# SSD stage of a hybrid encoder: ScalarE adds the decay differences, VectorE takes the minimum of four heads at once

## Chip, cores and metric

One core of a Trainium2 chip runs the whole program in one launch. The metric is device time in microseconds (us); lower is better. Engines are named as the profile names them: PE is TensorE (PEld its weight loads), DVE is VectorE, ACT is ScalarE, POOL is GpSimd, SP issues most DMAs.

## What is computed

Two layers on 1024 tokens of width 1024: dilated attention, then a bidirectional Mamba-2 SSD layer. The change lies in the SSD layer. For each of 8 groups (4 heads each) and each of 8 chunks (128 tokens each), with `acs` the running sum of `dt*a` inside a chunk, the reference does for each direction:

```
seg = acs_t[..., :, None] - acs_t[..., None, :]
decay = jnp.exp(jnp.where(lower, seg, -jnp.inf))
cb = jnp.einsum('bclgn,bcsgn->bcgls', cc, bc)
y_diag = jnp.einsum('bcgrls,bcsgrp->bclgrp', cb[:, :, :, None] * decay, xdt)
...
y_off = jnp.einsum('bclgn,cbgrpn->bclgrp', cc, prev) * jnp.exp(acs)[..., None]
```

The kernel handles both directions in one 128 x 128 matrix per head. The exponent is the smaller of the forward and the backward difference; each is the right one in its own triangle.

## The kernel before

**Work.** The main stream on PE is a dense projection: for each group six blocks (x0, x1, B, C, z0, z1) of 8 steps, each step six 128x512 matmuls (L376 to L378; each operand is split in a high part, cast by ACT in L271 into `whi`, and a low part, subtracted by DVE in L272 into `wlo`). A block accumulates in two of four PSUM banks `acc`. When it ends, ACT copies the two banks out with the convolution's middle tap (L1322), and DVE adds the other four taps (two instructions each, L1330), read from the same banks; only then are the banks free for the block after next. Later ACT applies silu (L1334).

**SSD items.** `ssd_items(g)` makes a list of small items, which `balance` weaves between the dense steps of the next group: A1 (PE transposes, L1403, copied out by ACT, L1405 and L1407), A2 (chunk states, L1415 to L1426), and for each chunk c from 7 down to 0: B0 (a DMA of the row sums into `acs`), B1(c), M(c) and, two chunks later, B2(c) (the output matmuls L1478, DVE L1482, POOL L1486). Each item carries a cost on PE and on DVE, and `balance` puts an item out when the DVE cost so far is small enough against the PE cost so far.

**B1(c)** of before: four DVE instructions make E (L1440: add a per-row scalar `delta`, take the minimum with the other direction's row sums); PE multiplies B by C (L1443); DVE masks the product into `cb` (L1446); ACT takes the exponential of E, head by head (L1448), scales `cb` into W, head by head (L1450), and takes the exponential of the row sums `acs` (L1452). **M(c)**: DVE adds the backward half into W (L1462, four instructions), multiplies E by W (L1464) and `acs` by C (L1467). After chunk 0 of a group ACT loads the table set for silu (L1454). Each engine runs its own instructions strictly in the order in which they are written.

Of the kernel before, what the change touches and what calls it, by code (L numbers as in the profile page):

```python
# [14 lines left out]
AF = mybir.ActivationFunctionType  # L15
OP = mybir.AluOpType
# [75 lines left out]
class Trunk:  # L92
# [1293 lines left out]
    def ssd_items(self, g):  # L1386
        nc = self.nc
# [6 lines left out]
        def ck(c):  # L1394
            return slice(P * c, P * c + P)
# [32 lines left out]
        def B0(c):  # L1428
            a = live["a", c] = self.u("acs", [P, 2, 4, P], F32, 4)
            nc.sync.dma_start(a, self.acsd[c, :, hs][None].to_broadcast([P, 2, 4, P]))  # L1430

        def dirs(c):

            return [d for d, k in ((0, c > 0), (1, c < C - 1)) if k]

        def B1(c):
            a = live["a", c]
            E, W = live["G", c] = self.u("E", [P, 4, P], F32, 3), self.u("W", [P, 4, P], F32, 2)
            for h in range(4):
                nc.vector.scalar_tensor_tensor(E[:, h], a[:, 0, h], self.delta[:, c, 4 * g + h:4 * g + h + 1], a[:, 1, h],  # L1440
                                               op0=OP.add, op1=OP.min)
            p = self.bank("a0", [P, P], 2)
            nc.tensor.matmul(p, st["B"][:, ck(c)], st["C"][:, ck(c)], start=True, stop=True)  # L1443
            cb = live["cb", c] = self.u("cb", [P, 2, P])
            tri = self.cst[:, CST["upper"][0]:CST["lower"][1]].rearrange("p (d l) -> p d l", d=2)
            nc.vector.tensor_mul(cb, p[:, None].to_broadcast([P, 2, P]), tri)  # L1446
            for h in range(4):
                nc.scalar.activation(E[:, h], E[:, h], AF.Exp, bias=self.nacb[:, c, 4 * g + h:4 * g + h + 1])  # L1448
            for h in range(4):
                nc.scalar.activation(W[:, h], cb[:, 0], AF.Copy, scale=self.dt[:, c, 4 * g + h:4 * g + h + 1])  # L1450
            ds = slice(dirs(c)[0], dirs(c)[-1] + 1)
            nc.scalar.activation(a[:, ds], a[:, ds], AF.Exp)  # L1452
            if c == 0 and g < 7:
                nc.scalar.preload_act_table_set(SILU)  # L1454

        def M(c):

            cb = live.pop(("cb", c))
            E, W = live["G", c]
            for h in range(4):  # L1460
                hh = 32 + 4 * g + h
                nc.vector.scalar_tensor_tensor(W[:, h], cb[:, 1], self.dt[:, c, hh:hh + 1], W[:, h],  # L1462
                                               op0=OP.mult, op1=OP.add)
            nc.vector.tensor_mul(E, E, W)  # L1464
            ds = dirs(c)
            a = live["a", c][:, ds[0]:ds[-1] + 1].rearrange("p d h l -> p (d h) l")
            nc.vector.tensor_mul(a, a, st["C"][:, None, ck(c)].to_broadcast([P, 4 * len(ds), P]))  # L1467

        def B2(c):

            y = self.bank("a3" if c % 2 else "a2", [P, 2, P])
            G, _ = live.pop(("G", c))
            ea = live.pop(("a", c))
            for r in range(2):
                mms = [(SS[6 - c if d else c - 1][:, d], ea[:, d]) for d in dirs(c)] + [(xt[c], G)]
                for k, (w, m) in enumerate(mms):
                    for i in range(2):
                        nc.tensor.matmul(y[64 * i:64 * i + 64, r], w[:, 2 * r + i], m[:, 2 * r + i],  # L1478
                                         start=k == 0, stop=k == len(mms) - 1)
            t = self.u("yt", [P, 2, P], F32, 2)  # L1480
            for r in range(2):
                nc.vector.scalar_tensor_tensor(t[:, r], st[f"x{r}"][:, ck(c)], self.sv[:, 2 * g + r:2 * g + r + 1],  # L1482
                                               y[:, r], op0=OP.mult, op1=OP.add)
            for r in range(2):
                z = st[f"z{r}"][:, ck(c)]
                nc.gpsimd.tensor_mul(z, z, t[:, r])  # L1486
            if c == 0 and g == 7:
                self.ylast = [st["z0"], st["z1"]]
            elif c == 0:
                for r in range(2):  # L1490
                    nc.gpsimd.dma_start(self.yd[2 * g + r], st[f"z{r}"])
# [7 lines left out]
        items = []  # L1499
# [6 lines left out]
        if g == 7:  # L1506
            items.append((1500, lambda: None, 0, 0))
        for c in range(C - 1, -1, -1):
            items.append((900, lambda c=c: B1(c), 0.25, 1.6))
            if c < C - 2:  # L1510
                items.append((500, lambda c=c: B2(c + 2), 1.7, 0.6))
            if c:
                items.append((1, lambda c=c: B0(c - 1), 0, 0))
            items.append((1150, lambda c=c: M(c), 0, 3.0))
# [273 lines left out]
```

## Time and profile before

| what | value |
|---|---|
| median of 3 runs | 1902.2 us (1900.9 to 1903.83) |
| the profiled execution | 1903.41 us, its span 1901.6 us |
| mean granted PE clock | 0.976 |
| busy share of the span | PE 94%, PEld 77%, DVE 75%, ACT 50%, POOL 17% |

The profile is of one execution. Busy shares are averages over stages with different limits. A wait in the trace is the idle time of an engine before an instruction, with the engine and line that ended it. "x4" behind a row means four instructions in a row, with the time from the first's start to the last's end. The SSD items run from about 1000 to about 1745 us; groups 1 to 5 look alike, about 93 us each, and the rows below are mostly of group 2.

### The profile page before, as it was taken

How to read it: one execution, taken by the hardware profiler on the slowest of the kernel's cores; microseconds unless marked ns; L12 is line 12 of the kernel's file. 1: busy time of each engine (PE TensorE's matmuls, PEld its weight loads, DVE VectorE, ACT ScalarE, POOL GpSimd, SP SyncE). 2: the span in 40 equal slices, each digit the busy share in tenths (PEclk: the TensorE clock that was granted, in tenths of full speed). 3: DMA queues.
4: the chain of work that ended last, by engine and by line, in shares of the span. 5: the costliest groups of instructions: out<-in, count | busy, mean ns of one | idle time of the engine just before them, and what ended most of it. 6: DMA issues, size and time to landing. Idle time of an engine off the chain costs nothing.

```text
span 1901.6 us, 28474 instructions
## 1 busy us (share of the span) xinstructions
PE 1790.2 (94%) x10050; PEld 1462.0 (77%) x10050; DVE 1428.1 (75%) x3220; ACT 955.5 (50%) x2095; POOL 330.1 (17%) x492
## 2 busy tenths in 40 slices
PE   5899999999999999999979999999999999888997
PEld 3678788777788887779868887878787877666787
DVE  8867568667664665566778898989898989878875
ACT  5454445444454545444435656464655555465632
POOL 4611122112211311000100101010101000233310
PEclk7899999999999999999989999999999999988998
DMA  6242234222311321355113232424232323244643
GB/s 254 87 130 81 81 107 134 85 86 83 105 52 54 81 60 49 91 188 169 63 45 99 85 100 78 100 78 101 78 110 80 106 83 91 89 129 127 199 155 101
DMA packets 99733, 193.65 MB, mean 102 GB/s; under 512 B 15624, under 2 KB 23048, under 8 KB 99592
## 3 DMA queue, kind: packets, MB, share of 16 engines
q1 hardware_dynamic: 86600, 167.32, 28.3%
q0 software_dynamic: 12288, 23.86, 4.5%
q8 instruction: 79, 1.29, 0.3%
q10 hardware_dynamic: 704, 0.66, 0.1%
q14 instruction: 62, 0.51, 0.1%
HBM read 169.00 MB, written 16.48 MB: 98 GB/s over the span
## 4 chain that ended last, share of the span: by engine, by line
PE 40%; DVE 7%; ACT 5%; issue 3%; DMA 2%; SPq 0%; DVEq 0%; POOL 0%; ACTq 0%; POOLq 0%
PE acc L376 8%; PE acc L378 7%; PE acc L377 7%; PE a L1478 3%; PE a L1416 2%; PE a L1002 2%; PE a L1000 2%; PE a L1001 2%; PE acc L1002 2%; PE acc L1001 1%; PE acc L1000 1%; DVE big L1330 1%; DVE wlo L272 1%; PE a L1403 1%; DMA acs<-acsd 1%
## 5 line engine op out<-in xcount | busy, mean ns | idle before, releaser
L376 PE MATMUL acc<-big,whi 128*128 128x512 f32 (+1 forms) x1520 | 632.7, 416 | 36.2 <-DVE big L1330 23.9
L377 PE MATMUL acc<-big,whi 128*128 128x512 f32 (+1 forms) x1520 | 597.3, 393 | 4.0 <-DVE big L294 4.0
L378 PE MATMUL acc<-big,wlo 128*128 128x512 f32 (+1 forms) x1520 | 597.2, 393 | 0.3 <-DVE wlo L272 0.3
L376 PEld LDWEIGHTS acc<-big,whi 128*128 128x128 f32 x1520 | 289.0, 190 | 103.7 <-issue 31.5
L378 PEld LDWEIGHTS acc<-big,wlo 128*128 128x128 f32 x1520 | 288.6, 190 | 64.8 <-DVE wlo L272 1.1
L377 PEld LDWEIGHTS acc<-big,whi 128*128 128x128 f32 x1520 | 290.1, 191 | 55.3 <-DVE big L294 7.5
L272 DVE TENSOR_TENSOR wlo<-wraw,whi 128x512 fp32r<-128x512 f32 (+1 forms) x298 | 216.8, 732 | 82.3 <-ACT whi L271 78.9
L271 ACT CAST whi<-wraw 128x512 fp32r<-128x512 f32 (+1 forms) x302 | 180.9, 611 | 86.1 <-PE a L1001 29.7
L695 ACT ACTIVATE sm<-sm,nb 128x256 f32<-128x256 f32 (+1 forms) x192 | 89.3, 466 | 198.3 <-DVE nb L693 195.7
L1448 ACT ACTIVATE E<-E,nacb 128x128 f32<-128x128 f32 x256 | 81.8, 391 | 200.2 <-DVE E L1440 200.2
L1486 POOL TENSOR_TENSOR big<-big,yt 128x128 f32<-128x128 f32 x128 | 68.0, 552 | 602.5 <-DVE yt L1482 547.5
L1330 DVE SCALAR_TENSOR_TENSOR big<-acc,cv,big 128x512 f32<-128x512 f32 (+1 forms) x248 | 170.9, 742 | 0.9 <-ACT big L1322 0.9
L706 DVE COPY pt<-a 128x512 f32<-128x512 f32 (+1 forms) x96 | 57.6, 600 | 76.5 <-PE a L704 76.5
L690 DVE CUSTOM_DVE_ANT_0 sm<-a,cst 128x256 f32<-128x256 f32 (+1 forms) x192 | 65.0, 376 | 62.4 <-PE a L685 62.0
L1001 PE MATMUL acc<-big,whi 128*128 128x512 f32 x224 | 91.4, 408 | 9.7 <-DVE big L1553 7.2
L1000 PE MATMUL a<-big,whi 128*128 128x256 f32 (+1 forms) x304 | 100.1, 329 | 0.0
L1002 PE MATMUL a<-big,wlo 128*128 128x256 f32 (+1 forms) x304 | 98.7, 325 | 0.7 <-DVE wlo L272 0.7
L1001 PE MATMUL a<-big,whi 128*128 128x256 f32 (+1 forms) x304 | 98.5, 324 | 0.0
L1002 PE MATMUL acc<-big,wlo 128*128 128x512 f32 x224 | 91.8, 410 | 4.6 <-DVE wlo L272 4.4
L1000 PE MATMUL acc<-big,whi 128*128 128x512 f32 x224 | 92.7, 414 | 1.2 <-ACT big L271 1.2
L592 POOL DMA_DIRECT2D rt<-kT x92 | 50.4, 561 | 249.4 <-ACT kT L532 149.9
L1462 DVE SCALAR_TENSOR_TENSOR W<-cb,dt,W 128x128 f32<-128x128 f32 x256 | 82.7, 379 | 7.3 <-ACT W L1450 6.6
(254 smaller groups left out, 3149.0 us busy)
## 6 DMA issues: line engine op xcount, KB each, us to landing
wraw<-in_win SPq DMA_DIRECT2D x186, 256.0 KB
acs<-acsd SPq DMA_DIRECT2D x64, 512.0 KB
wraw<-in_wout SPq DMA_DIRECT2D x112, 256.0 KB
big<-in_modw SPq DMA_DIRECT2D x48, 512.0 KB
yd<-big POOLq DMA_DIRECT2D x14, 512.0 KB, 3.5
big<-yd SPq DMA_DIRECT2D x28, 256.0 KB
vT<-mix POOLq DMA_DIRECT2D x20, 256.0 KB, 5.0
big<-in_xT SPq DMA_DIRECT2D x8, 512.0 KB
```

The costliest lines, as they stand in the source:

```text
L271: self.nc.scalar.copy(dst_hi, src)
L272: self.late.append((lambda: self.lo_engine.tensor_sub(dst_lo, src, dst_hi.bitcast(F32)), tile))
L376: mm(o, hi[:, cols], x_[:, t0:t0 + n], start=first, stop=False, **kw)
L377: mm(o, hi[:, cols], x_[:, H2 + t0:H2 + t0 + n], start=False, stop=False, **kw)
L378: mm(o, lo[:, cols], x_[:, t0:t0 + n], start=False, stop=last, **kw)
L695: nc.scalar.activation(sm[:, h, :W], sm[:, h, :W], AF.Exp, bias=nb[:, h:h + 1], scale=0.125, accum_out=stat[:, h, 1, i:i + 1])
L1000: mm(o, hi[:, c], x[:, t:t + n], start=kt == 0 and (n == H2 or m % 2 == 0), stop=False, **kw)
L1001: mm(o, hi[:, c], x[:, H2 + t:H2 + t + n], start=False, stop=False, **kw)
L1002: mm(o, lo[:, c], x[:, t:t + n], start=False, stop=kt == nkt - 1, **kw)
L1330: nc.vector.scalar_tensor_tensor(y[:, lo:hi], a[:, lo + o:hi + o], w[:, cv, k:k + 1], y[:, lo:hi], op0=OP.mult, op1=OP.add)
L1448: nc.scalar.activation(E[:, h], E[:, h], AF.Exp, bias=self.nacb[:, c, 4 * g + h:4 * g + h + 1])
L1462: nc.vector.scalar_tensor_tensor(W[:, h], cb[:, 1], self.dt[:, c, hh:hh + 1], W[:, h], op0=OP.mult, op1=OP.add)
```

## The change

The four DVE instructions of B1 that added and took the minimum become four ACT instructions that only add (`Identity` with a bias), and one DVE instruction that takes the minimum for all four heads. This minimum now stands behind the mask `cb` on DVE. On ACT the scaling into W now stands ahead of the exponential of E. The planner's DVE cost of B1 falls from 1.6 to 1.1.

```diff
@@ B1
             for h in range(4):
-                nc.vector.scalar_tensor_tensor(E[:, h], a[:, 0, h], self.delta[:, c, 4 * g + h:4 * g + h + 1], a[:, 1, h],
-                                               op0=OP.add, op1=OP.min)
+                nc.scalar.activation(E[:, h], a[:, 0, h], AF.Identity, bias=self.delta[:, c, 4 * g + h:4 * g + h + 1])
             p = self.bank("a0", [P, P], 2)
             nc.tensor.matmul(p, st["B"][:, ck(c)], st["C"][:, ck(c)], start=True, stop=True)
             cb = live["cb", c] = self.u("cb", [P, 2, P])
             tri = self.cst[:, CST["upper"][0]:CST["lower"][1]].rearrange("p (d l) -> p d l", d=2)
             nc.vector.tensor_mul(cb, p[:, None].to_broadcast([P, 2, P]), tri)
+            nc.vector.tensor_tensor(E, E, a[:, 1], op=OP.min)
+            for h in range(4):
+                nc.scalar.activation(W[:, h], cb[:, 0], AF.Copy, scale=self.dt[:, c, 4 * g + h:4 * g + h + 1])
             for h in range(4):
                 nc.scalar.activation(E[:, h], E[:, h], AF.Exp, bias=self.nacb[:, c, 4 * g + h:4 * g + h + 1])
-            for h in range(4):
-                nc.scalar.activation(W[:, h], cb[:, 0], AF.Copy, scale=self.dt[:, c, 4 * g + h:4 * g + h + 1])
@@ items
-            items.append((900, lambda c=c: B1(c), 0.25, 1.6))
+            items.append((900, lambda c=c: B1(c), 0.25, 1.1))
```

In the changed kernel L1440 is the ACT addition, L1445 the mask `cb`, L1446 the minimum, L1448 the scaling into W and L1450 the exponential of E; all other lines keep their numbers.

The planner's new cost moves items too. On ACT, in group 2 from the first chunk (c = 7) on, before:

```order
L1448 ACTIVATE E_11386<-E_11386,nacb_8966 128x128 x4
L1450 ACTIVATE W_11387<-cb_11394,dt_8962 128x128 x4
L1452 ACTIVATE acs_11288<-acs_11288 128x512
L1322 ACTIVATE big_11411<-acc_11280,cv_8789 128x512
L1322 ACTIVATE big_11411<-acc_11281,cv_8789 128x512
```

and after the change:

```order
L1322 ACTIVATE big_11408<-acc_11285,cv_8789 128x512
L1322 ACTIVATE big_11408<-acc_11286,cv_8789 128x512
L1440 ACTIVATE E_11411<-acs_11304,delta_8965 128x128 x4
L1448 ACTIVATE W_11412<-cb_11419,dt_8962 128x128 x4
L1450 ACTIVATE E_11411<-E_11411,nacb_8966 128x128 x4
L1452 ACTIVATE acs_11304<-acs_11304 128x512
```

The chunk's work on ACT has moved from ahead of the two copies of a block's end to behind them. For chunk 3 (L1440 right behind two L1322) and chunk 0 the order against L1322 is as before, with the four additions put in.

On DVE, at the same place, before:

```order
L1440 SCALAR_TENSOR_TENSOR E_11386<-acs_11288,delta_8965 128x128 x4
L1446 TENSOR_TENSOR cb_11394<-a_2085_11392,cst_71 128x256
L1462 SCALAR_TENSOR_TENSOR W_11387<-cb_11394,dt_8962,W_11387 128x128 x4
L1464 TENSOR_TENSOR E_11386<-E_11386,W_11387 128x512
L1467 TENSOR_TENSOR acs_11288<-acs_11288,big_11029 128x512
L1330 SCALAR_TENSOR_TENSOR big_11411<-acc_11280,cv_8789,big_11411 128x512
```

and after, where three further L1330 stand in place of the "...":

```order
L1445 TENSOR_TENSOR cb_11419<-a_2086_11417,cst_71 128x256
L1446 TENSOR_TENSOR E_11411<-E_11411,acs_11304 128x512
L1330 SCALAR_TENSOR_TENSOR big_11408<-acc_11285,cv_8789,big_11408 128x512
...
L272 TENSOR_TENSOR wlo_11444<-wraw_11216,whi_11443 128x512
L1462 SCALAR_TENSOR_TENSOR W_11412<-cb_11419,dt_8962,W_11412 128x128 x4
L1464 TENSOR_TENSOR E_11411<-E_11411,W_11412 128x512
L1467 TENSOR_TENSOR acs_11304<-acs_11304,big_11044 128x512
```

M(7) has moved behind the first four taps of the block and one L272.

At the end of the group ACT has, before:

```order
L1322 ACTIVATE big_11951<-acc_11837,cv_8789 128x512
L1448 ACTIVATE E_11954<-E_11954,nacb_8966 128x128 x4
L1450 ACTIVATE W_11955<-cb_11962,dt_8962 128x128 x4
L1452 ACTIVATE acs_11881<-acs_11881 128x512
L1454 ACT_TABLE_LOAD
```

and after:

```order
L1322 ACTIVATE big_11974<-acc_11859,cv_8789 128x512
L1440 ACTIVATE E_11977<-acs_11904,delta_8965 128x128 x4
L1448 ACTIVATE W_11978<-cb_11985,dt_8962 128x128 x4
L1450 ACTIVATE E_11977<-E_11977,nacb_8966 128x128 x4
L1452 ACTIVATE acs_11904<-acs_11904 128x512
L1454 ACT_TABLE_LOAD
```

Four additions have been put between the block's copy and the table load.

## Rows read from the trace of the kernel before

**Rows 1.** Busy time by stretch; columns PE, PEld, DVE, ACT, POOL, clock, DMA share, GB/s.
```profile
1200.00:1250.00 50.00, 48.47 (x297) 39.71 (x296) 47.27 (x104) 31.41 (x75) 5.03 (x10) 1.00 0.38 98
...
1700.00:1750.00 50.00, 42.98 (x264) 33.15 (x263) 48.51 (x87) 32.08 (x72) 25.17 (x22) 0.90 0.42 130
```

**Rows 2.** PE's waits from 1000 to 1750 us: total us, times, longest.
```profile
PE acc L376 <- DVE big L1330: 12.4, 8, 1.7
...
PE a L1403 <- ACT bt L1407: 6.8, 7, 1.2
```

**Rows 3.** Groups of instructions, 1000 to 1750 us: busy us, mean ns, idle before.
```profile
L1440 DVE SCALAR_TENSOR_TENSOR E<-acs,delta 128x128 f32<-128x128 f32 x256 | 76.6, 361 | 6.6 <-DMA acs<-acsd 6.6
...
L1464 DVE TENSOR_TENSOR E<-E,W 128x512 f32<-128x512 f32 x64 | 45.3, 707 | 2.2
```

**Rows 4.** Timeline of chunk 2, group 2: start us, us, engine, line; DVE, ACT, PE.
```profile
1237.06 1.13 DVE L1440 SCALAR_TENSOR_TENSOR E<-acs,delta 128x128 f32<-128x128 f32 x4
...
1239.12 1.35 DVE L1462 SCALAR_TENSOR_TENSOR W<-cb,dt,W 128x128 f32<-128x128 f32 x4
1241.11 1.22 DVE L1467 TENSOR_TENSOR acs<-acs,big 128x1024 f32<-128x1024 f32 x1
1242.25 1.40 DVE L1330 SCALAR_TENSOR_TENSOR big<-acc,cv,big 128x510 f32<-128x510 f32 x2
...
1237.52 1.28 ACT L1448 ACTIVATE E<-E,nacb 128x128 f32<-128x128 f32 x4 [6.00 <-DVE E L1440]
1238.70 1.27 ACT L1450 ACTIVATE W<-cb,dt 128x128 f32<-128x128 f32 x4
1239.88 1.05 ACT L1452 ACTIVATE acs<-acs 128x1024 f32<-128x1024 f32 x1
...
1243.14 0.47 PE L376 MATMUL acc<-big,whi 128*128 128x512 f32 x1 [1.53 <-DVE big L1330]
```

**Rows 5.** Timeline of DVE, chunks 7 to 3 of the same group; last row ACT.
```profile
1200.99 1.23 DVE L1462 SCALAR_TENSOR_TENSOR W<-cb,dt,W 128x128 f32<-128x128 f32 x4 [0.47 <-ACT W L1450]
...
1203.72 2.72 DVE L1330 SCALAR_TENSOR_TENSOR big<-acc,cv,big 128x512 f32<-128x512 f32 x4 [0.18 <-ACT big L1322]
...
1209.88 0.42 DVE L1446 TENSOR_TENSOR cb<-a,cst 128x256 f32<-128x256 f32 x1 [0.47 <-PE a L1443]
...
1215.05 1.14 DVE L1440 SCALAR_TENSOR_TENSOR E<-acs,delta 128x128 f32<-128x128 f32 x4
...
1221.24 1.13 DVE L1440 SCALAR_TENSOR_TENSOR E<-acs,delta 128x128 f32<-128x128 f32 x4
...
1226.52 0.69 DVE L272 TENSOR_TENSOR wlo<-wraw,whi 128x512 fp32r<-128x512 f32 x1
...
1232.51 2.71 DVE L1330 SCALAR_TENSOR_TENSOR big<-acc,cv,big 128x512 f32<-128x512 f32 x4
...
1226.26 1.46 ACT L1322 ACTIVATE big<-acc,cv 128x512 f32<-128x512 f32 x2 [0.65 <-PE acc L378]
```

**Rows 6.** Timeline of ACT and PE at the end of the group.
```profile
1255.62 1.45 ACT L1322 ACTIVATE big<-acc,cv 128x512 f32<-128x512 f32 x2 [6.58 <-issue]
1256.96 1.27 ACT L1448 ACTIVATE E<-E,nacb 128x128 f32<-128x128 f32 x4
...
1259.94 1.28 ACT L1454 ACT_TABLE_LOAD   x1
1261.23 2.95 ACT L1334 ACTIVATE big<-big 128x1024 f32<-128x1024 f32 x3
...
1264.24 0.66 PE L1403 MATMUL a<-cst,big 128*128 128x128 f32 x4 [0.32 <-ACT big L1334]
1266.13 1.02 PE L1403 MATMUL a<-cst,big 128*128 128x128 f32 x6 [1.23 <-ACT bt L1407]
```

**Rows 7.** Timeline of PE: one wait in group 6, one in group 7.
```profile
1605.60 0.47 PE L376 MATMUL acc<-big,whi 128*128 128x512 f32 x1 [1.75 <-DVE big L1330]
...
1675.10 0.50 PE L1002 MATMUL acc<-big,wlo 128*128 128x512 f32 x1 [2.48 <-DVE wlo L272]
```

## The prediction

> **What bounds the kernel now.** I read the busy time by stretch first, because the page's average (DVE 75%) mixes stages. In a middle group PE is busy 48.47 of 50 us, DVE 47.27 and ACT only 31.41; in the last group DVE is busy 48.51 and PE 42.98 [rows 1]. So in groups 1 to 5 (some 465 us) PE sets the pace, and a change on DVE or ACT counts only where PE waits; in the last two groups DVE sets it. Next the waits of PE. In the whole stage there are two kinds that matter: eight waits, 12.4 us, for a convolution tap (L1330) that frees a PSUM bank, and seven, 6.8 us, at the transposes that open the next group [rows 2]. Then the timeline of one middle group, to see what is late at each. The tap wait comes behind chunk 2: DVE reaches that tap at 1242.25, and PE, which had been waiting 1.53 us, starts at 1243.14 [rows 4]; groups 1 to 5 have one such wait each of about this size. The transposes wait for ACT: silu for 0.32 us, then the copies behind it for 1.23 us [rows 6]. The question is therefore not how busy DVE is, but when it reaches that tap, and when ACT reaches silu.
>
> **Cost of the operations.** The four DVE instructions take 1.05 us from the first to the mask behind them (the row's 1.13 us less the overlap of its end). Their mean over the stage is 361 ns each, idle not counted [rows 3]. The minimum of 128x512 is not in the trace; the nearest row is the product of E and W, two SBUF operands of the same size and type, 707 ns [rows 3], and about 0.61 us from its start to the next instruction when nothing interferes. I take 0.61; the bounds are 0.55 (half of an acs product, 1.14/2 [rows 4]) and 0.71. DVE is thus relieved of 0.44 us per chunk, 28 us over 64 chunks. The addition on ACT is a 128x128 activation with a bias, as the exponential is: four of those take 1.18 us (1237.52 to 1238.70 [rows 4]). ACT thus gets 64 times 1.18, 75 us, where it is idle for a third of the time. Both sums say little until one sees which chunks carry them to PE.
>
> **A chunk with nothing between B1 and M (chunks 5, 4, 2 and in part 3).** Before: DVE starts E at 1237.06, ACT its exponential 0.46 later, then W 1.18 later, and DVE can't add to the last head of W until ACT has it (the four take 1.35 instead of 1.13); it reaches the next work at 1242.25, 5.19 us after the start [rows 4]. After: from the mask, ACT starts W after 0.46 (the same handing over), the exponential 1.18 later, that of `acs` another 1.17 later, lasting 1.05; then 0.06 to hand over and 1.14 for the product with C: 5.06 us. DVE saves 0.44 us of work and mostly spends it waiting for ACT, since W has moved forward and the exponential backward in a chain of the same length. Gain 0.13 per such chunk. This needs the additions to be done in the ACT idle time that stands ahead (6.00 us here [rows 4]); without it they cost up to 1.18.
>
> A rule of the Trainium skill speaks for more than that: VectorE: DVE Perf Modes, section on the TRN2 errata, says that each SBUF instruction pays a fixed extra latency and that tiles of 512 elements or more should be used to spread it. The trace agrees that one 128x512 is cheaper than four 128x128 [rows 3]. By that rule alone the stage would give back 28 us of DVE; the second rival below takes it up from rows.
>
> **The tap wait, groups 1 to 5.** I follow DVE from the first tap of the block (1203.72 [rows 5]) to the tap on which PE waits. Chunk 7 now stands behind the block's copies on ACT: the additions end about 1203.2, so the minimum ends at 1203.85, and that first tap starts 0.13 later than before. Work of M(7), 2.4 us (1200.99 to 1203.72 less its pauses [rows 5]), now lies behind the taps instead of ahead: +2.4. The low part L272 waits for a cast that now comes after chunk 7: +0.15. Chunk 6 saves its 0.44 and the 0.47 that its mask waited for PE [rows 5]: -1.0 with rounding. Chunk 5 took 6.19 (1215.05 to 1221.24) with an L272 in it; now 0.61 + 5.06: -0.5. Chunk 4 took 5.28: -0.2 [rows 5]. Chunk 3 has the block's copies ahead of it on ACT (L1322 at 1226.26 [rows 5]), so its additions cannot be early: the chain on ACT, cast, copies, additions, W, two exponentials, makes 6.35 of its 5.99 (1226.52 to 1232.51 [rows 5]): +0.4. Chunk 2: -0.1. Sum +1.15: PE's wait grows from 1.5 to about 2.65. Lower bound: all gains of 0.44 come through and M(7) costs nothing, and the wait goes: -1.5. Upper bound: chunks 6 to 2 each pay half of the 1.18 as well: +4.
>
> **The end of a group.** Chunk 0 stands on ACT between the block's last copies, which wait for PE (1255.62), and the table load (1259.94 [rows 6]). The additions have no idle time ahead of them here. E starts at 1256.96 right behind the copies [rows 6], so the four additions push W, the exponentials, table load and silu by 1.18. W's place does not save anything, since only ACT's own order counts. PE's first wait grows from 0.32 to 1.5, and the second, behind the same ACT queue, stays 1.23: +1.17 in each of the five groups. The product that the last output matmuls need moves by about 0.4 us and has over 1 us in hand. Bounds: 0, if ACT had an unseen idle time, and 1.5.
>
> Groups 1 to 5 together: 5 x (1.15 + 1.17) = +11.6. Group 0 has neither wait of this size, and its last chunk has idle time ahead on ACT: 0.
>
> **Groups 6 and 7.** DVE sets the pace, and PE waits for it, 1.75 us at 1605.60 [rows 7]. In every other chunk of group 6, and in nearly all of group 7, taps or other DVE work lie between B1 and M and cover ACT's chain, so the whole 0.44 is gained. Group 6: its first chunk behind a copy costs 1.15, then three at 0.44, two at 0.13 and 0.5 for the short last one: -0.9. Group 7: the first chunk's additions stand in the ACT queue ahead of a cast whose low part PE already awaits (2.48 us at 1675.10 [rows 7]): +1.2; then six at 0.44: -2.6. Together -2.3, between -5 and +1.
>
> **Sum.** +11.6 - 2.3 = +9.3 us. The profiled execution took 1903.41 us (span 1901.6), 1.2 above the median of 1902.2; I add the change to the median: **1911 us**, 0.5% slower. Measured differences of this kernel tell from no change above about 0.2%, or 3.8 us.
>
> **Rivals.**
> *Forecast: a longer ACT queue costs more than DVE gives back.* 1904 to 1918. For it: the five group ends, where nothing can hide the additions. Against it: the tap term is a long sum of small shifts. Chance 0.55.
> *DVE's relief reaches PE.* If the 0.44 of five chunks or more arrives at the tap (2.2 is more than the 1.5 that PE waits), the eight tap waits go: -12.4 [rows 2]; groups 6 and 7 give -5; the group ends still cost up to +5.9. That gives 1885 to 1897. It decides from the point where the additions are always early and M(7) does not matter. Against it: the 5.06 us chain in a chunk, of which DVE's own work is the smaller part. Chance 0.20.
> *They cancel.* The tap wait stays at 1.5, the group ends cost 5.9 and the last groups give back 5: within 4 us of 1902. Chance 0.17.
> *ACT becomes the limit in each chunk.* If the additions are not early, because the row sums land late or the queue is never idle ahead, chunks 6 to 2 lose 0.5 each on top, 2.5 per group in five groups: 1923 or so. Against it: idle times of up to 6 us in the ACT rows. Chance 0.08.
>
> **How the numbers follow.** Slower by over 0.2%: forecast and last rival, 0.63. Same: 0.17. Faster: 0.20. The range runs from 1897 to 1919: it leaves out most of the second rival and the far end of the last, some 2 in 10. The likeliest case alone spans 1904 to 1918.
>
> **What would show it.** In the changed kernel's profile: four additions in 1.18 us and a minimum of about 0.61 to 0.7 us; waits of PE for L1330 of some 2.6 us in groups 1 to 5, sum near 18; waits of the transposes for silu near 1.5 us five times; DVE pauses before the products of M that end on ACT; an ACT addition that starts right behind L1322 at chunks 7, 3 and 0. I am wrong if the tap wait shrinks, if ACT is idle just ahead of chunk 0's additions at a group's end, or if the period of a middle group is not some 2 us above 93.

## The result, and the profile after

The changed kernel takes 1919.93 us (median of 4 runs, 1915.65 to 1925.54) against 1903.01 us for the kernel before on the same chip: ratio 1.0100, 95% interval 1.0074 to 1.0126. It is slower by 16.9 us, 0.9% of the median before, 8.9 us above the forecast of 1911 and 0.9 us above the upper end of the range. The profiled execution took 1915.65 us (span 1913.9, mean clock 0.975), the fastest of the four.

Busy time by stretch in the changed kernel, columns as in [rows 1]:

```profile
1200.00:1250.00 50.00, 47.64 (x293) 38.81 (x292) 43.40 (x84) 38.88 (x105) 4.60 (x10) 1.00 0.37 100
1700.00:1750.00 50.00, 43.24 (x270) 32.19 (x268) 46.46 (x79) 42.72 (x108) 26.43 (x21) 0.93 0.53 147
```

The relief of DVE is there: 47.27 us busy in the middle stretch became 43.40, 48.51 in the last became 46.46. PE did not get busier; in the middle stretch it fell from 48.47 to 47.64.

PE's waits of the changed kernel from 1000 to 1750 us (total, times, longest), and the groups of instructions that are new, moved or waiting (busy us, mean ns, idle before):

```profile
PE acc L376 <- DVE big L1330: 16.0, 6, 4.7
...
PE a L1403 <- ACT big L1334: 6.2, 10, 0.6
```

```profile
L1440 ACT ACTIVATE E<-acs,delta 128x128 f32<-128x128 f32 x256 | 81.6, 392 | 13.3 <-DMA acs<-acsd 13.3
...
L1446 DVE TENSOR_TENSOR E<-E,acs 128x512 f32<-128x512 f32 x64 | 44.2, 691 | 31.7 <-ACT E L1440 31.7
L1445 DVE TENSOR_TENSOR cb<-a,cst 128x256 f32<-128x256 f32 x64 | 26.8, 419 | 32.7 <-PE a L1442 32.7
```

The operations cost what was forecast: an addition 392 ns, the minimum 691 ns. But DVE now idles 31.7 us ahead of the minimum, for the additions, and 32.7 us ahead of the mask, for PE (11.8 before). Of PE's waits in [rows 2] those for the tap rose from 12.4 to 16.0 us: in groups 1 to 5 five waits of 1.54 became five of 2.26, and in group 6 three, 4.7 us together, became one of 4.66. Those for silu (L1334), 1.9 us before, are now 6.2.

**Where the time went.** I measure a group from one table load at a group's end (L1454) to the next. Before, group 2 took 92.65 us (1167.29 to 1259.94), after, 94.87 (1168.03 to 1262.90; groups 2, 4 and 5, without a fall of the clock, 94.87 to 94.93). In the profiled executions: up to the first L1344 (the table load that opens group 0), ahead of any changed instruction, -3.0 us; group 0, +2.0 (65.15 to 67.17); groups 1 to 5, +10.7 (466.6 to 477.3); group 6, +5.1 (87.04 to 92.11); from there to the end, -2.5. Sum +12.3, the difference of the spans.

Chunks 3 and 2 of group 2 in the changed kernel: ACT, DVE, PE. They answer to [rows 4, 5].

```profile
1227.38 1.44 ACT L1322 ACTIVATE big<-acc,cv 128x512 f32<-128x512 f32 x2
1228.71 1.27 ACT L1440 ACTIVATE E<-acs,delta 128x128 f32<-128x128 f32 x4
1229.88 1.27 ACT L1448 ACTIVATE W<-cb,dt 128x128 f32<-128x128 f32 x4
1231.06 1.27 ACT L1450 ACTIVATE E<-E,nacb 128x128 f32<-128x128 f32 x4
1232.23 1.05 ACT L1452 ACTIVATE acs<-acs 128x1024 f32<-128x1024 f32 x1
...
1228.74 0.42 DVE L1445 TENSOR_TENSOR cb<-a,cst 128x256 f32<-128x256 f32 x1
1230.01 0.69 DVE L1446 TENSOR_TENSOR E<-E,acs 128x512 f32<-128x512 f32 x1 [0.85 <-ACT E L1440]
...
1234.49 2.72 DVE L1330 SCALAR_TENSOR_TENSOR big<-acc,cv,big 128x512 f32<-128x512 f32 x4
...
1239.04 0.42 DVE L1445 TENSOR_TENSOR cb<-a,cst 128x256 f32<-128x256 f32 x1
...
1244.07 1.40 DVE L1330 SCALAR_TENSOR_TENSOR big<-acc,cv,big 128x510 f32<-128x510 f32 x2
...
1227.84 0.38 PE L1442 MATMUL a<-big,big 128*128 128x128 f32 x2
...
1244.96 0.47 PE L376 MATMUL acc<-big,whi 128*128 128x512 f32 x1 [2.26 <-DVE big L1330]
```

Chunk 3 is the first place to look at: the additions start right behind the block's copies (1228.71), the minimum waits 0.85 us for them, and the taps start 6.65 us after PE's B times C (1227.84 to 1234.49). Chunk 2 has idle time ahead of its additions; mask to tap takes 5.03 us (1239.04 to 1244.07), where 5.06 was forecast.

A shorter stop of PE stands behind chunk 6, where M(7) now lies behind the block's first taps:

```profile
1212.58 1.40 DVE L1330 SCALAR_TENSOR_TENSOR big<-acc,cv,big 128x510 f32<-128x510 f32 x2
...
1213.47 0.47 PE L376 MATMUL acc<-big,whi 128*128 128x512 f32 x1
```

PE starts this matmul 0.50 us after the one ahead of it (1212.97), where 0.23 is usual, and 0.89 us after DVE began the last two taps, as at the tap wait of chunk 2 (1244.07 to 1244.96). The change has this stop in each of the groups 1 to 5; with its instructions at the places of before (e2_engines_only below) no group has it.

The end of the group, ACT and PE, which answers to [rows 6]:

```profile
1257.41 1.45 ACT L1322 ACTIVATE big<-acc,cv 128x512 f32<-128x512 f32 x2 [5.69 <-issue]
1258.75 1.27 ACT L1440 ACTIVATE E<-acs,delta 128x128 f32<-128x128 f32 x4
1259.92 1.28 ACT L1448 ACTIVATE W<-cb,dt 128x128 f32<-128x128 f32 x4
...
1262.90 1.28 ACT L1454 ACT_TABLE_LOAD   x1
...
1266.25 0.33 PE L1403 MATMUL a<-cst,big 128*128 128x128 f32 x1 [0.61 <-ACT big L1334]
1267.20 0.65 PE L1403 MATMUL a<-cst,big 128*128 128x128 f32 x4 [0.62 <-ACT big L1334]
```

From the copies' start to the table load ACT takes 5.49 us where it took 4.32 [rows 6], and PE waits 0.61 and 0.62 us for silu, 1.23 together, instead of 0.32.

Group 6, where the forecast failed; DVE, ACT, PE:

```profile
1580.41 0.42 DVE L1445 TENSOR_TENSOR cb<-a,cst 128x256 f32<-128x256 f32 x1 [1.90 <-PE a L1442]
...
1586.90 0.69 DVE L1446 TENSOR_TENSOR E<-E,acs 128x512 f32<-128x512 f32 x1 [1.31 <-ACT E L1440]
...
1591.35 2.72 DVE L1330 SCALAR_TENSOR_TENSOR big<-acc,cv,big 128x512 f32<-128x512 f32 x4
...
1584.27 1.44 ACT L1322 ACTIVATE big<-acc,cv 128x512 f32<-128x512 f32 x2
1585.60 1.27 ACT L1440 ACTIVATE E<-acs,delta 128x128 f32<-128x128 f32 x4
...
1601.81 0.76 PE L376 MATMUL acc<-big,whi 128*128 128x512 f32 x1 [4.66 <-DVE big L1330]
1602.37 0.63 PE L377 MATMUL acc<-big,whi 128*128 128x512 f32 x1
```

Chunks 7 and 6 follow each other without a gap on ACT: the copies come behind chunk 7's exponentials, chunk 6's additions behind the copies, its minimum waits 1.31 us, and the taps begin at 1591.35. PE waits 4.66 us for the last of them, and its next matmul takes 0.63 us instead of 0.39: the clock has fallen to the lower level.

The windows of the whole of group 6: before, the change, and the change with the places of before in this group alone (e12_g6_places below):

```profile
1539.47:1626.51 87.04, 79.43 (x504) 65.06 (x498) 78.86 (x173) 49.88 (x116) 8.24 (x18) 1.00 0.33 92
1549.15:1641.26 92.11, 81.94 (x484) 66.72 (x483) 76.27 (x149) 59.25 (x148) 8.50 (x18) 0.94 0.32 86
1557.24:1643.92 86.68, 78.49 (x484) 64.13 (x483) 75.65 (x149) 59.28 (x148) 8.28 (x18) 1.00 0.34 92
```

DVE's busy time did fall, from 78.86 to 76.27 us, but the group grew by 5.1: PE is busy 2.5 us longer, at a mean clock of 0.94 instead of 1.00, and idle 2.6 us longer (7.6 to 10.2). Its clock records show 10.2 us at 1.2 GHz: 6.8 behind the wait of 4.66, and 3.4 at the group's opening, behind the end of group 5. Before has none.

### The profile page after: what moved, and what is told of

Read it like the earlier page. It is cut to its first block, busy times and chain, and to the rows that moved or that the text cites. A ratio compares the mean times of both kernels' runs of the same rounds, so it can differ in the third digit from the quotient of the medians.

```text
span 1913.9 us, 28575 instructions
## 1 busy us (share of the span) xinstructions
PE 1795.6 (94%) x10050; PEld 1463.4 (76%) x10050; DVE 1395.6 (73%) x3028; ACT 1027.5 (54%) x2351; POOL 325.3 (17%) x492
## 4 chain that ended last, share of the span: by engine, by line
PE 37%; ACT 9%; DVE 6%; issue 3%; DMA 2%; SPq 0%; DVEq 0%; POOL 0%; ACTq 0%; POOLq 0%
PE acc L376 7%; PE acc L378 6%; PE acc L377 6%; PE a L1416 3%; PE a L1478 3%; PE a L1002 2%; PE a L1000 2%; PE a L1001 2%; ACT E L1450 2%; ACT W L1448 2%; PE acc L1002 1%; PE acc L1000 1%; PE acc L1001 1%; DVE big L1330 1%; DMA acs<-acsd 1%
## 5 line engine op out<-in xcount | busy, mean ns | idle before, releaser
L272 DVE TENSOR_TENSOR wlo<-wraw,whi 128x512 fp32r<-128x512 f32 (+1 forms) x298 | 214.7, 725 | 79.2 <-ACT whi L271 75.5
L1330 DVE SCALAR_TENSOR_TENSOR big<-acc,cv,big 128x512 f32<-128x512 f32 (+1 forms) x248 | 171.1, 743 | 0.0
L1448 ACT ACTIVATE W<-cb,dt 128x128 f32<-128x128 f32 x256 | 81.7, 391 | 94.2 <-DVE cb L1445 94.2
L1322 ACT ACTIVATE big<-acc,cv 128x512 f32<-128x512 f32 x62 | 44.6, 771 | 87.1 <-PE acc L378 58.5
```

What stands on the lines that cost most here:

```text
L272: self.late.append((lambda: self.lo_engine.tensor_sub(dst_lo, src, dst_hi.bitcast(F32)), tile))
L1330: nc.vector.scalar_tensor_tensor(y[:, lo:hi], a[:, lo + o:hi + o], w[:, cv, k:k + 1], y[:, lo:hi], op0=OP.mult, op1=OP.add)
```

## The experiments

**Theories.** T1: what costs is ACT's queue, above all where the additions stand behind a block's copies (chunks 7, 3, 0). T2: what costs are the places that the planner gives the items at cost 1.1. A third cause is mixed into both, falls of the clock behind PE's waits. So I read three things in each profile beside the time: the period of a middle group without a fall, the tap wait of groups 1 to 5, and the wait for silu at their ends. The silu wait is the sum of the waits for L1334 at one end. "Falls" counts, within the windows of groups 1 to 5, the tap waits and the group ends that a stretch at 1.2 GHz followed; one behind the end of group 5 lies in group 6. Ratios are to runs of the kernel before on the same chip.

| kernel | median us | ratio (95% interval) | period us | tap wait us | silu wait us | group 6 us | falls: taps, ends |
|---|---|---|---|---|---|---|---|
| before | 1900.9 to 1903.6 | 1 | 92.65 | 1.54 | 0.32 | 87.0 | 0, 1 |
| the change | 1919.93 | 1.0100 (1.0074 to 1.0126) | 94.90 | 2.26 | 1.23 | 92.1 | 1, 0 |
| e1_place_only | 1917.98 | 1.0079 (1.0066 to 1.0091) | 93.05 | 1.95 | 0.32 | 89.9 | 4, 2 |
| e2_engines_only | 1917.88 | 1.0086 (1.007 to 1.0103) | 94.51 | 2.25 | 1.23 | 87.9 | 3, 2 |
| e3_c0_old | 1931.6 | 1.0146 (1.0127 to 1.0164) | 94.80 | 2.27 | 1.13 | 95.5 | 2, 1 |
| e4_early_add | 1923.93 | 1.0101 (1.0085 to 1.0116) | none | 2.26 | 0.32 | 91.7 | 5, 2 |
| e5_swap_only | 1946.52 | 1.0239 (1.0219 to 1.0259) | none | 4.48 | 1.13 | 93.1 | 5, 2 |
| e6_730_old | 1899.94 | 0.9996 (0.9983 to 1.0009) | 92.47 | 1.38 | 0.32 | 88.7 | 0, 0 |
| e7_3_old | 1909.43 | 1.0041 (1.0026 to 1.0056) | 93.65 | 1.38 | 1.23 | 88.7 | 0, 3 |
| e8_no_swap | 1939.18 | 1.0207 (1.0181 to 1.0232) | none | 3.42 | 1.23 | 88.3 | 5, 3 |
| e9_g6_old | 1899.06 | 0.9992 (0.9981 to 1.0003) | 92.47 | 1.38 | 0.32 | 86.2 | 0, 0 |
| e10_tail | 1894.69 | 0.9966 (0.9954 to 0.9978) | 92.08 | 0.98 | 0.32 | 84.7 | 0, 0 |
| e11_730_old_cost11 | 1909.54 | 1.0043 (1.0031 to 1.0055) | 92.80 | 1.70 | 0.32 | 91.0 | 0, 2 |
| e12_g6_places | 1916.09 | 1.0072 (1.0056 to 1.0087) | 94.90 | 2.26 | 1.23 | 86.7 | 2, 1 |

("none": each of the five had a fall. Periods, waits and falls are those of the profiled executions. Line numbers behind the edit are a few higher in some of the kernels. Group 6 holds time at 1.2 GHz too: 13.7 us in e3_c0_old, 10.2 in the change and e5_swap_only, 6.8 in e4_early_add and e11_730_old_cost11, 3.4 in e1_place_only, e2_engines_only, e6_730_old, e7_3_old and e8_no_swap, none in the rest.)

**Places alone.** The kernel before with the planner's cost of the change.

```diff
-            items.append((900, lambda c=c: B1(c), 0.25, 1.6))
+            items.append((900, lambda c=c: B1(c), 0.25, 1.1))
```

> The instructions of before, at the places of the change (planner cost 1.1). Theory 1 (ACT's longer queue costs, the places hardly): within 4 us of before, 1900 to 1907. Theory 2 (the places cost: chunk 7's M behind the block's taps, and the new order in groups 0 and 6): M(7) alone is priced at 2.4 us at each of five tap waits, and group 6 at 5, so 1915 to 1920, with tap waits (L1330) of 3 us and more in groups 1 to 5 and one of over 4 us in group 6. My prediction's own sum for this kernel: +2.4 x 5 = 12, 1914.

Two of its middle groups, one with falls and one without:

```profile
1360.44:1456.88 96.44, 92.73 (x538) 75.70 (x534) 80.87 (x175) 51.93 (x121) 8.35 (x18) 0.96 0.33 88
1456.88:1549.93 93.05, 89.55 (x538) 73.23 (x534) 80.85 (x175) 51.84 (x120) 8.40 (x18) 1.00 0.31 91
```

The time agrees with T2 (+14), but not the make-up. The tap wait grows by 0.4 us only, not by 2.4, the period by 0.40, and the wait in group 6 is 3.37 us, not over 4. The rest is group 6 (+2.9) and the clock: six falls in groups 1 to 5 where before had one, each about 1.6 us (94.6 us is a group with one, 93.05 with none).

**Engines alone.** The change with the cost put back to 1.6; each item stands where it stood before.

```diff
-            items.append((900, lambda c=c: B1(c), 0.25, 1.1))
+            items.append((900, lambda c=c: B1(c), 0.25, 1.6))
```

> The instructions of the change, at the places of before (planner cost 1.6). Theory 1: slow as the change, 1915 to 1920, and PE waits of 1.2 us for silu (L1334) at each group's end. Theory 2: only the group ends' 1.17 x 5 = 6 us remain, and the tap wait shrinks by 2.4 of its 2.3, so 1900 to 1905. In both the wait for silu stays at 1.2 us; the tap wait of groups 1 to 5 tells them apart: 2.3 by theory 1, under 0.5 by theory 2.

The tap wait stays at 2.25 us: T1, for groups 1 to 5. The periods add up: instructions +1.86, places +0.39 (0.40 above), together +2.25 in the change. But the 0.40 above lies in the tap wait, and the 0.39 here does not, since the tap wait is the same with and without the places; some 0.3 of it is the stop behind chunk 6. The times do not add up (each alone costs 14 us, both 17); in the profiled executions the falls differ, six with places alone, five here, one in the change.

**Chunk 0 without additions.** The change; chunk 0 keeps the four DVE instructions, and the order of ACT stays that of the change.

```diff
+            if c:
                 for h in range(4):
                     nc.scalar.activation(E[:, h], a[:, 0, h], AF.Identity, ...)
+            else:
+                for h in range(4):
+                    nc.vector.scalar_tensor_tensor(E[:, h], a[:, 0, h], ..., a[:, 1, h], op0=OP.add, op1=OP.min)
...
+            if c:
                 nc.vector.tensor_tensor(E, E, a[:, 1], op=OP.min)
```

> The change, but chunk 0 of each group keeps the four VectorE instructions, so that ScalarE's queue at a group's end is as short as before. By the term for the group end (+1.17 each) PE's wait for silu falls from 1.23 to 0.3 us and the kernel gains 5 x 0.9 to 5 x 1.17 on the change, -4.5 to -6: 1914 to 1915. Rival: another wait takes its place (VectorE reaches chunk 0's products later, or the copies that follow silu are late anyway): within 2 us of the change.

A miss: the silu wait falls only to 1.13. The edit had left W ahead of the exponential, so W now waits for a mask that waits for E on DVE; it put in what it took out. The median is 12 us above the change, though the waits of groups 1 to 5 are nearly the same; its runs show clocks of 0.964 to 0.971 against 0.970 to 0.975, and its profile has 27.3 us at 1.2 GHz in groups 1 to 6 against 13.6. Why the clock fell more often here stays open.

**Additions early.** They are issued at the end of M of the chunk before.

```diff
-            for h in range(4):
-                nc.scalar.activation(E[:, h], a[:, 0, h], AF.Identity, ...)   # in B1(c)
...
+            if c:
+                B1a(c - 1)   # at the end of M(c): the four additions of chunk c - 1
```

> The change, with the additions of chunk c issued at the end of chunk c+1's M (those of chunk 7 ahead of the last state update), so that on ScalarE they stand ahead of the block's copies and of the waits in B1. If the place in ScalarE's queue is what costs (theory 1): the wait for silu returns to 0.3 us and the additions behind the copies at chunks 7 and 3 go, -1.2 and -0.4 or more in five groups, 1905 to 1912. If the places of B1 and M cost (theory 2): only the group end's gain, 1914 to 1916. Risk: the addition waits at the head of ScalarE's queue for the row sums' transfer, and holds the exponentials or copies behind it; then 1920 or more, with ScalarE waiting on the DMA.

Chunk 3 of group 2 here, ACT and DVE:

```profile
1232.39 1.05 ACT L1456 ACTIVATE acs<-acs 128x1024 f32<-128x1024 f32 x1
...
1233.84 1.28 ACT L1440 ACTIVATE E<-acs,delta 128x128 f32<-128x128 f32 x4
1235.03 1.43 ACT L1322 ACTIVATE big<-acc,cv 128x512 f32<-128x512 f32 x2
1236.35 1.27 ACT L1452 ACTIVATE W<-cb,dt 128x128 f32<-128x128 f32 x4
...
1238.83 0.69 DVE L1468 TENSOR_TENSOR E<-E,W 128x512 f32<-128x512 f32 x1 [0.57 <-ACT E L1454]
```

Half right. At the group's end the silu wait is 0.32 again. At chunk 3 nothing is won: ACT comes straight from chunk 4's exponentials, so the additions now push the copies instead of W, and the tap wait is 2.26 as before. Between chunks 4 and 3 ACT has no idle time on either side of the copies. Group 2 took 96.43 us with two falls, about 93.2 without; all five tap waits were followed by one, and the time is no better. 1923.93 us lies where the risk in the text above put it, but hardly for its reason: ACT waits 20.1 us in all for the row sums ahead of the additions, 13.3 in the change.

**The swap alone.** The kernel before, W ahead of the exponential of E on ACT.

```diff
-            for h in range(4): nc.scalar.activation(E[:, h], E[:, h], AF.Exp, ...)
             for h in range(4): nc.scalar.activation(W[:, h], cb[:, 0], AF.Copy, ...)
+            for h in range(4): nc.scalar.activation(E[:, h], E[:, h], AF.Exp, ...)
```

> The kernel before, with the one edit that on ScalarE the scaling into W stands ahead of the exponential of E. VectorE keeps its four instructions and no additions exist. If the swap is what lengthens ScalarE's chain at chunk 0 (W has to wait for the mask, which waits for E on VectorE): the wait for silu (L1334) rises from 0.32 to 1.1 us or more, as it does with chunk 0's old instructions behind a swapped order, +0.8 x 5 = 4, 1907 or so. If the swap is free: within 3 us of before and a silu wait of 0.32.

Chunk 2 of group 2, DVE, ACT and PE:

```profile
1246.57 1.13 DVE L1440 SCALAR_TENSOR_TENSOR E<-acs,delta 128x128 f32<-128x128 f32 x4
1247.62 0.42 DVE L1446 TENSOR_TENSOR cb<-a,cst 128x256 f32<-128x256 f32 x1
...
1252.64 1.40 DVE L1330 SCALAR_TENSOR_TENSOR big<-acc,cv,big 128x510 f32<-128x510 f32 x2
...
1248.07 1.28 ACT L1448 ACTIVATE W<-cb,dt 128x128 f32<-128x128 f32 x4 [6.72 <-DVE cb L1446]
...
1253.53 0.77 PE L376 MATMUL acc<-big,whi 128*128 128x512 f32 x1 [4.48 <-DVE big L1330]
```

The swap is anything but free: 44 us, where some 5 were expected; the text had foreseen the silu wait (1.13) and not the tap wait (4.48). E, mask, W, two exponentials and the product now stand in one line, 6.07 us (1246.57 to 1252.64) against 5.19 [rows 4]. With the additions moved off DVE and the minimum behind the mask, at the same places, 14 of the 44 us are left (engines alone): E no longer stands ahead of the mask.

**No swap.** The change at the places of before, with the minimum ahead of the mask and the exponential ahead of W. Against the kernel before:

```diff
             for h in range(4):
-                nc.vector.scalar_tensor_tensor(E[:, h], a[:, 0, h], ..., a[:, 1, h], op0=OP.add, op1=OP.min)
+                nc.scalar.activation(E[:, h], a[:, 0, h], AF.Identity, ...)
+            nc.vector.tensor_tensor(E, E, a[:, 1], op=OP.min)
```

> At the places of before: additions on ScalarE and minimum on VectorE in all chunks, but in the order of before (minimum ahead of the mask, the exponential of E ahead of W). If the swap is what the change needs: at chunks 3 and 0, where the additions come late, the minimum (0.6 us and two hand-overs) now stands in ScalarE's chain, tap wait 2.25 + 0.7 and silu wait 1.23 + 0.7, period about 96, 1925. If the swap only costs: tap wait and silu wait fall below 2.25 and 1.23, period under 94.5, 1912 or less.

The first of the two by the tap wait (3.42 us) and the time (1939 us, 14 above what was expected); the silu wait stays 1.23, where 1.9 was expected. At chunk 3 of group 2 the minimum waits 1.50 us for the additions, and the mask stands behind it. So neither half of the change is cheaper alone at these places, and with late additions the minimum must not stand ahead of the mask.

**Old instructions at chunks 7, 3 and 0.** At the places of before, these three as before, in the second kernel chunk 3 alone.

```diff
+            if c in (7, 3, 0):   # the second kernel: (3,)
+                for h in range(4): nc.vector.scalar_tensor_tensor(E[:, h], a[:, 0, h], ..., a[:, 1, h], ...)
+            else:
                 for h in range(4): nc.scalar.activation(E[:, h], a[:, 0, h], AF.Identity, ...)
... (and the order behind the mask, chunk by chunk, as before or as in the change)
```

> At the places of before: chunks 7, 3 and 0 (those whose additions stand behind a block's copies on ScalarE) in the instructions and the order of before, chunks 6, 5, 4, 2 and 1 in those of the change. Theory A (only the additions behind copies cost; the rest of the chain is no longer than before): silu wait back to 0.32 and tap wait back to 1.4 (the 0.17 that chunk 2 gained), so the undisturbed period of a middle group is 92.5 us against 94.5 with all chunks changed and 92.65 before: 1900 to 1906. Theory B (each changed chunk costs on ScalarE): the tap wait stays over 2 us and the period near 94, 1910 or more. Falls of the clock may add 1.5 us each to either.

> At the places of before: only chunk 3 in the instructions and the order of before. Theory A: the tap wait behind chunk 2 is set by chunk 3's queue on ScalarE, counted from the block's end on TensorE, so it falls from 2.25 to about 1.4 us; the silu wait stays 1.23. Undisturbed period 94.5 - 0.85 = 93.6; in time 4 us less than with all chunks changed, 1914. Theory B (several chunks add up to the tap wait, as my prediction's sum has it: chunk 3 carries 0.4 of it): the tap wait falls by 0.4 at most.

The windows of a middle group of each, first chunk 3 alone, then 7, 3 and 0 (the first number is its length):

```profile
1262.84:1356.49 93.65, 89.81 (x533) 73.39 (x533) 78.54 (x154) 59.98 (x149) 8.93 (x18) 1.00 0.34 91
```

```profile
1258.39:1350.86 92.47, 89.55 (x538) 73.31 (x535) 79.44 (x160) 57.73 (x140) 8.93 (x18) 1.00 0.34 92
```

Theory A of both texts. Chunk 3 alone takes the tap wait from 2.25 to 1.38 and the period from 94.51 to 93.65; chunks 7 and 0 take the silu wait from 1.23 to 0.32 and the period to 92.47. At the places of before the additions of chunk 7 do not stand behind copies (in the kernel with chunk 3 old they start at 1284.35 us, the copies at 1298.98, behind that chunk's exponentials), so copies stand ahead at chunks 3 and 0 only. Chunks 7 and 0 were not tried apart; that the 1.18 us is chunk 0's is read from where it shows, at the group's end. What is left, five changed chunks of eight, is 0.18 better than before, and the time is the same. With chunk 3 alone the time came out 5 us below the 1914 expected.

**Group 6.** The same, with chunk 6 of group 6 old too; and then, in the changed chunks, ACT's exponential of `acs` ahead of that of E and DVE's product with C ahead of that of E and W.

```diff
+        old = (7, 6, 3, 0) if g == 6 else (7, 3, 0)
...
             nc.scalar.activation(W ...)
+            nc.scalar.activation(a[:, ds], a[:, ds], AF.Exp)      # second kernel only
             nc.scalar.activation(E ..., AF.Exp)
-            nc.scalar.activation(a[:, ds], a[:, ds], AF.Exp)
...
-            nc.vector.tensor_mul(E, E, W)
             nc.vector.tensor_mul(a, a, st["C"] ...)
+            nc.vector.tensor_mul(E, E, W)                         # second kernel only
```

> As the kernel with chunks 7, 3 and 0 in the old instructions (at the places of before), and in group 6 chunk 6 in the old ones too, since there its additions stand behind a block's copies and its minimum waits 1.33 us for them. If that is what makes group 6 88.7 us against 87.0 before: the wait of 2.0 us in it falls to 1.25 or less and the group to 87.5, 1 us less in time than without, 1899. Rival: VectorE sets the pace in group 6, and the four instructions come back to it: no change.

> As the kernel before this one in the list, and in the changed chunks ScalarE takes the exponential of the row sums ahead of that of E, and VectorE the product with C ahead of the product of E and W, so that the shorter product (0.61 against 1.14 us) is what remains behind ScalarE's chain. If that chain sets the time from mask to tap in a chunk: it falls from 5.03 to 4.56, the tap wait from 1.38 to 0.9 and the period of a middle group from 92.5 to 92.0: 2.5 us less, 1896. Rival: VectorE's own work (4.56 with its starts) or TensorE's chunk rows set it: tap wait stays at 1.38.

Chunk 2 of group 2 in the second, DVE and PE:

```profile
1236.32 0.42 DVE L1451 TENSOR_TENSOR cb<-a,cst 128x256 f32<-128x256 f32 x1
...
1239.20 1.21 DVE L1479 TENSOR_TENSOR acs<-acs,big 128x1024 f32<-128x1024 f32 x1
1240.34 0.68 DVE L1481 TENSOR_TENSOR E<-E,W 128x512 f32<-128x512 f32 x1
1240.94 1.39 DVE L1330 SCALAR_TENSOR_TENSOR big<-acc,cv,big 128x510 f32<-128x510 f32 x2
...
1241.82 0.47 PE L376 MATMUL acc<-big,whi 128*128 128x512 f32 x1 [0.98 <-DVE big L1330]
```

With chunk 6 old as well, the wait of 2.00 us in group 6 fell to 1.22, as expected. The group is 2.4 us shorter (88.66 to 86.22), but a fall of 3.4 us at the opening of group 6 stands in the first profile and not in the second, an estimated 1.6 of it; in time the two kernels can't be told apart. With the short product last, mask to tap takes 4.62 us (1236.32 to 1240.94), the tap wait falls to 0.98 and the kernel is faster than both: 1894.69 us, ratio 0.9966.

**The places once more.** Chunks 7, 3 and 0 old, at the places of the change; and the change with the places of before in group 6 alone.

```diff
-            items.append((900, lambda c=c: B1(c), 0.25, 1.1))
+            items.append((900, lambda c=c: B1(c), 0.25, 1.6 if g == 6 else 1.1))   # the second kernel
```

> Chunks 7, 3 and 0 in the old instructions, at the places of the change (planner cost 1.1). If places and instructions add up as in the four kernels so far: undisturbed period 92.5 + 0.4 = 92.9, tap wait 1.8, group 6 some 2 to 3 us longer (a wait of 3.4 us in it, as at these places with the instructions of before); 1905 to 1910, where the higher end comes from falls of the clock behind the tap waits. If the places only cost together with the additions behind copies: 1900, as at the places of before.

> The change, with the planner cost of B1 at 1.6 in the last woven group alone, so that only there chunks 7 and 6 stand at the places of before. If these places are what made group 6 5.1 us longer (a wait of 4.66 us behind a tap, and a fall of the clock after it): the wait falls to 2.0 and the group to 87.9 as in the kernel with all places of before, the change gets 3 to 4.5 us faster, 1915 to 1917; groups 1 to 5 keep their 94.9 and 2.26. If ScalarE's additions make group 6 longer wherever they stand: 92 us and no change.

PE's longest wait in group 6, first kernel and second:

```profile
PE acc L376 <- DVE big L1330: 5.2, 2, 4.3
```

```profile
PE acc L376 <- ACT E L1440: 4.3, 3, 2.0
```

As expected both times. The places cost 0.3 us in the period and, in group 6, a wait of 4.3 us; with the places of before there alone, the wait is 2.00 us, group 6 takes 86.7 us where the change took 92.1, and the median is 1916.09. The wait follows the places. The gain in time is less sure: the intervals of the two ratios overlap, and the two profiled executions take the same time (1915.95 and 1915.65 us), with three falls in groups 1 to 5 here and one in the change. (In the order of instructions it is B1 of chunks 7, 5 and 4 that moves there, by one, two and one dense steps, not 7 and 6.)

## Why the prediction was wrong

Its sign and most of its sum were right; the step that failed is the one that begins "Group 6: its first chunk behind a copy costs 1.15" and ends at -0.9, where the runs showed +5.1. Term by term, from the profiled executions and the periods:

| step | forecast | measured |
|---|---|---|
| minimum, additions, chunk of 5.06 us | 0.61 to 0.71, 1.18, 5.06 | 691 ns busy, 1.17, 5.03 |
| tap part of a middle group | +1.15 | +1.07 (0.86 + 0.39 - 0.18), of it +0.72 in the tap wait |
| end of a group | +1.17 | +1.18 (chunks 7 and 0) |
| groups 1 to 5 | +11.6 | +10.7 |
| group 0 | 0 | +2.0 |
| group 6 | -0.9 | +5.1 |
| from there to the end | -1.4 | -2.5 |

The measured terms add up to +15.3; with the -3.0 ahead of any changed instruction they give the difference of the two spans. The medians differ by 16.9, since the profiled execution of the change is its fastest, 4.3 us below its median, and that of before lies 0.4 above its own.

**Group 6.** I took DVE to set the pace and counted 0.44 for most chunks (seven of the eight are in the sum). DVE's busy time did fall by 2.6 us, but the group did not follow. At the places of the change chunk 7 runs right into chunk 6 and the copies, and PE waits 4.66 us at once where it had waited 4.7 us in three parts; the tap waits as such hardly grew. What grew is the rest: 2.5 us of PE's busy time at the lower clock, and 2.6 us of idle time, of it 0.9 for silu. Behind the waits of 4.27 to 4.66 us that the change, e3_c0_old, e4_early_add and e11_730_old_cost11 have here, the clock was at 1.2 GHz for 6.8 us each time; behind the 2.00 us of four kernels with the places of before it did not fall. With those places in group 6 alone, and no fall in it, the group is 0.4 us shorter than before, near the forecast -0.9. So the new places lengthened the wait, and much of the time behind it is the clock's. The other 3.4 us at 1.2 GHz, behind the end of group 5, come ahead of these places. That I had worked out the new places for groups 1 to 5, and for group 6 only as "its first chunk behind a copy", is the gap.

**Group 0.** With the places alone it grows by 0.2, with the instructions alone by 0.9. Of its +2.0, 0.70 is a wait of PE for ACT at 1030.29 that no group had before. The rest may be the marker itself, the table load, which chunk 0's additions put later; that is not shown.

**The tap part was right by compensation, that is, by luck.** The list itself adds up to 1.28 with the 0.13 at its head, which the sum left out. It had M(7) behind the taps at +2.4; the places cost 0.39 or 0.40, in the change as a short stop behind chunk 6 and not at the tap wait at all. Nearly all that happens ahead of chunk 3 is forgotten there: in the change the copies start 0.05 us after PE's end of the block, and the additions behind them. Chunk 3, where I had +0.4, has 0.86, and the reliefs of chunks 6, 5, 4 and 2, some -1.8 in my list, come to -0.18 together with chunk 1. So the way I went, "I follow DVE from the first tap of the block", was too long: the way from PE's last release is what counts.

**The clock.** No term of the sum had it. The median of the change lies 4.3 us above its own profiled execution, whose clock is 0.975; one of the other runs shows 0.970. The kernel with chunk 0 old has the same undisturbed period as the change and a median 12 us above it; in the profiles it has twice the time at 1.2 GHz in groups 1 to 6, so the falls are a term of some us by themselves. How many of them an execution gets is not explained here.

**Rivals.** "DVE's relief reaches PE" is refuted for this order of instructions: the five chunks that keep it gain 0.18 us per group, 0.57 with the order of the last two products changed as well. "ACT the limit in each chunk" is right at chunk 3 and at the group's end alone. Two figures of the prediction do not follow from their own terms, and nothing above rests on them: the upper end of 1897 for DVE's relief (its terms give 1885 to 1891) and 0.55 for 1.14/2, which is 0.57.

The rule of the Trainium skill that the prediction weighed (VectorE: DVE Perf Modes, TRN2 errata: tiles of 512 elements or more spread the fixed latency) holds for the instruction, 691 ns against four of 361, but no run here shows a gain in time by it alone. Of moving work, the Trainium skill (Perfetto Trace Analysis, Optimizing Scalar/DVE Operations) says that handing some to ScalarE may make sense where the DVE is saturated; DVE was busy 47.27 of 50 us in the middle stretch [rows 1], so its condition looks met, and yet the work handed over gained 0.18 us per group where ACT had idle time ahead of it (e6_730_old), and cost where it had none: in this stretch PE, busy 48.47 of 50 us, set the pace.

## What to carry to other kernels

When work moves to a less busy engine, look at each place for what stands ahead of it in that engine's queue: the same additions cost nothing in five chunks and about a microsecond behind the copies that wait for PE (0.86 us at chunk 3, 1.18 at the group's end), so the change should be made place by place. Start a chain at the last thing the bounding engine released, and put the shortest instruction behind its last wait. After a planner's cost has changed, go through every stage with its own layout, not only the repeating one.

## What was not expected of the hardware

A wait of PE can cost more than itself. Over all fourteen kernels, in groups 1 to 5, none of the 30 tap waits of 0.98 to 1.72 us was followed by a fall of the clock, and 27 of the 40 of 1.94 to 4.48 us were. Such a fall, with places alone, behind a wait of 2.15 us (the stretch's windows, clock third from the end):

```profile
1438.00:1440.00 2.00, 1.48 (x5) 1.26 (x6) 2.00 (x5) 0.17 (x2) 0.00 (x0) 0.78 0.00 0
1440.00:1442.00 2.00, 2.00 (x13) 1.59 (x13) 1.10 (x4) 1.45 (x5) 0.00 (x0) 0.50 0.47 131
```

PE runs at 1.2 GHz for 3.4 us, about 1.6 us lost (94.62 us for a group with one such fall, 93.05 with none). Why the same wait of 2.26 us was followed by one five times in five with early additions and once in five in the profiled execution of the change is open.
